# GpSimd's element-wise instructions moved to VectorE in a two-layer hybrid attention, convolution and gating backbone

## The chip, the cores and the metric

The kernel runs on one core of one Trainium2 chip. The metric is device time in microseconds (us) of one execution. The engines are written as in the profile: PE is TensorE, with PEld for its weight loads, DVE is VectorE, ACT is ScalarE, POOL is GpSimd, and SP is SyncE, which issues the DMAs.

## The reference

Two layers work on 1024 latent tokens and 256 context tokens of width 1024. In each layer one combined input projection feeds three mixers: differential attention, a long convolution, and chunked spatial gating. Their outputs are gated, projected, merged and projected once more. Cut to what matters (per layer, latent part):

```python
h = rms_norm(x, norm_pre[l]) * (1.0 + sc[:, None]) + sh[:, None]
z = h @ w_in[l]
q = apply_rope(qk_heads(z[..., COL_Q:COL_GA]), cos, sin)
k = apply_rope(qk_heads(z[..., COL_K:COL_V]), cos, sin)
y_a = diff_head_out(diff_attend(q, k_all, v_all, lam), da_subln[l], lam_init)
filt = hyena_filter(n, hy_f_w1[l], hy_f_b1[l], hy_f_w2[l], hy_f_b2[l], hy_f_w3[l], hy_f_freq[l])
y_b = hyena_branch(z[..., COL_HY:COL_GB], hy_short_w[l], hy_short_b[l], filt, hy_bias[l])   # FFT convolution
y_c = gmlp_branch(z[..., COL_GM:COL_GC], gm_ln_g[l], gm_ln_b[l], gm_ws[l], gm_bs[l])
# merge: out = sum_i sigmoid(gate_i) * ((y_i * silu(g_i)) @ w_branch[l, i]);  out = out @ w_out[l]
x = x + gt[:, None] * rms_norm(out, norm_post[l])
```

The context tokens go through the same weights in the first layer; in the second they only give keys and values.

## The kernel before

Activations lie with channels on the 128 partitions and tokens along the free axis, in three chunks (512, 512 and 256 tokens). All large matmuls are taken as three products of split numbers (`mm3`, L180): high half of the weights by high half of the data, high by low, and low by high, one row of the profile each (L183, L184, L185). So each weight block of 128 x 1024 is loaded by a DMA (`wr`), copied by ACT to its high half `wh` (L103), and its low half is `wl = wr - wh` (L104). `Weights.split_to` does this one block ahead of use, with two buffers each for `wr`, `wh` and `wl`; the subtraction runs on GpSimd, but for some blocks named in `on_vector` on VectorE.

The stages, in order of time: **the start** (0 to 320 us: the long-convolution filters of layer 0, the conditioning and the first normalisation), **attention of layer 0** (to 905), **convolution and gating of layer 0** (to 1420), **merge** (`phase_m`, to 1680), **output** (`phase_o`, to 1870), and the same for layer 1: attention (to 2435), convolution and gating with the filters of layer 1 among them (to 2870), merge (to 3115) and output (to the end).

The change touches element-wise helpers of all these:

- `kvq`: the rotary step on keys and queries. VectorE makes a shuffled copy and a product (L396, L397), GpSimd a product and a sum (L398, L399).
- `filters` (L733), `butterfly` (L641), `fold` (L712): the filter in time (`hb`, L750), its sum of squares (`ssq`, L756), even and odd parts `U` (L760 on VectorE, L761 on GpSimd), then a hand-made radix-8 step (L650) of sums and differences named `Z`, `W` and `o`, most on VectorE, some on GpSimd by their number in `pool_share`. Its results go to PE as `fk` (filters) or `fu` (data), L699 to L704.
- `conv`, `product`, `inverse`, `conv_out`: the data side of the convolution. A short convolution makes `zc` (L791 to L793), a product of two of them (L831) is transposed on PE (`T`, L838).
- `mix` (L1091): the gating. VectorE normalises (`bst`, L193 to L195, `vn`, L1129), PE multiplies (`mm`, L1103), VectorE scales (`mv`, L1134), and GpSimd adds and multiplies (L1136, L1137).
- `phase_m`: products with the gates (`gy`, L1161) and accumulation (`acc`, L1182). `phase_o` and `phase_last`: the residual sum `xt` (L1235, L1325).

What sets the order: the helpers are Python generators that the phases interleave, and a list scheduler then sets each engine's queue when the program is built, from the dependencies and its own estimates. Each engine runs its queue strictly in order, and an instruction that waits for a semaphore holds what stands behind it.

Of the kernel before, what the change touches and what calls it, by code (L numbers as in the profile page):

```python
# [55 lines left out]
class Weights:  # L56


    def __init__(self, nc, pool, order, src):
        self.nc, self.pool, self.order, self.src = nc, pool, order, src  # L60
        self.on_vector = ({("out", 0, 2, d) for d in (1, 3, 5, 7)}
                          | {("br", 1, i, d) for i in range(3) for d in range(KT)})
        self.i = 0
# [106 lines left out]
class Kernel:  # L170
# [185 lines left out]
    def hmod(self, l, c, x):  # L356
# [5 lines left out]
        for k in range(KT):  # L362
# [8 lines left out]
            (nc.gpsimd if k in (1, 3, 5) else nc.vector).tensor_tensor(out=hl[:, k, :], in0=u, in1=hh[:, k, :].bitcast(F32),  # L371
                                                                op=SUB)
# [3 lines left out]
    def kvq(self, l, h, P, psum):  # L376
# [13 lines left out]
        def rope(c, ps):  # L390
# [7 lines left out]
            nc.gpsimd.tensor_tensor(out=sh, in0=sh, in1=St[:, t0:t0 + n], op=MUL)  # L398
            nc.gpsimd.tensor_tensor(out=t1, in0=t1, in1=sh, op=ADD)  # L399
# [241 lines left out]
    def butterfly(self, U, P, ZW, pool_share):  # L641
# [91 lines left out]
    def filters(self, l, q, P, M, psum, ZW):  # L733
# [6 lines left out]
        for i, (b0, b1, st) in enumerate(((0, 2, 1), (1, 3, 1), (4, 6, 2), (7, 5, 1))):  # L740
# [14 lines left out]
            if i:  # L755
                nc.gpsimd.tensor_tensor(out=ss, in0=ss, in1=sq, op=ADD)  # L756
# [115 lines left out]
    def conv_out(self, l, q, t0, n, y, u, x0, nrm):  # L872
# [3 lines left out]
        nc.gpsimd.tensor_tensor(out=y, in0=y, in1=x0, op=MUL)  # L876
# [3 lines left out]
    def inverse(self, Y, yt, M, P, psum):  # L880
# [7 lines left out]
        def tt(out, a, b, op, eng=nc.vector):  # L888
            eng.tensor_tensor(out=out, in0=a, in1=b, op=op)
# [30 lines left out]
        hh = tt(two(), cs[:, 5:7, :], cs[:, 0:4:3, :], SUB, nc.gpsimd)  # L920
# [77 lines left out]
    def ctx_conv(self, l, q, P, M, psum):  # L998
# [3 lines left out]
        nc.gpsimd.tensor_tensor(out=v, in0=v, in1=x1, op=MUL)  # L1002
# [88 lines left out]
    def mix(self, l, P, psum):  # L1091
# [19 lines left out]
        for i in range(nch):  # L1111
# [30 lines left out]
    def phase_m(self, l):  # L1142
        nc = self.nc
        with ExitStack() as st:
# [5 lines left out]
            for i in (0, 2, 1):  # L1150
                gat = {}
                for c in self.chunks(l):
# [3 lines left out]
                    for b in range(4):  # L1156
# [582 lines left out]
```

## Time and profile before

| | |
|---|---|
| median of 3 runs | 3230.13 us (3229.13 to 3231.52) |
| the profiled execution | 3228.0 us |
| its span in the trace | 3226.2 us |
| PE busy | 3016.2 us (93%) |
| VectorE busy | 1809.8 us (56%), 3822 instructions |
| ScalarE busy | 1224.0 us (38%) |
| GpSimd busy | 961.0 us (30%), 640 instructions |
| mean TensorE clock granted | 0.971 of full speed |

The span lies inside the execution; 1.8 us of the profiled execution lie around it. PE's busy time is the sum of its matmuls' time, which is longer where the granted clock is lower. An engine that is not busy waits for another one or for a DMA, or has nothing to do. In the views of waits, a row names the engine and line that waited, what ended the wait, the total in us, the number of waits and the longest.

### The profile page before, as it was taken

The numbers are of one execution on the slowest core, as the hardware profiler recorded it, in microseconds if no ns is written. First come the engines' busy times: TensorE is split into PE (matmuls) and PEld (weight loads), VectorE is DVE, ScalarE is ACT, GpSimd is POOL, SyncE is SP. The second block draws the span as 40 slices with busy tenths as digits, with TensorE's granted clock in tenths as the row PEclk, the third lists the DMA queues.
The fourth block names the chain that finished last, engine by engine and source line by source line (L and its number), as shares of the span: only waits on it lengthen the run. The fifth ranks groups of instructions, "written<-read, shape, count | busy, mean of one in ns | idle before, by whom it ended". The sixth has DMA issues, their size and how long they took to land. (4 is left out here: it accounts for less than half of the span.)

```text
span 3226.2 us, 43742 instructions
## 1 busy us (share of the span) xinstructions
PE 3016.2 (93%) x16220; PEld 2539.3 (79%) x16220; DVE 1809.8 (56%) x3822; ACT 1224.0 (38%) x2037; POOL 961.0 (30%) x640
## 2 busy tenths in 40 slices
PE   8888999999999998999999899999998888899998
PEld 4777878787878787878877778888886766788878
DVE  6754757676865655313355755545466667534344
ACT  5332535353532322223343444535454333323231
POOL 1442020202013333223543321221214544322431
PEclk9899999999999999999999999999999999999999
DMA  6323222222355555435452421221114645546342
GB/s 248 111 81 107 76 72 77 72 77 80 104 186 175 188 168 169 146 127 155 131 163 85 145 70 48 67 64 56 61 60 140 189 157 181 191 144 218 106 134 79
DMA packets 243381, 395.79 MB, mean 123 GB/s; under 512 B 23582, under 2 KB 127902, under 8 KB 241888
## 3 DMA queue, kind: packets, MB, share of 16 engines
q1 hardware_dynamic: 243168, 392.99, 37.7%
q8 instruction: 128, 2.10, 0.3%
q14 instruction: 85, 0.70, 0.1%
HBM read 285.81 MB, written 97.65 MB: 119 GB/s over the span
## 5 line engine op out<-in xcount | busy, mean ns | idle before, releaser
L183 PE MATMUL pd<-hh,wh 128*128 128x512 f32 (+1 forms) x2784 | 1052.2, 378 | 10.5 <-DVE r L397 6.4
L185 PE MATMUL pd<-hh,wl 128*128 128x512 f32 (+1 forms) x2784 | 1037.8, 373 | 2.2 <-POOL wl L104 2.2
L184 PE MATMUL pd<-hl,wh 128*128 128x512 f32 (+1 forms) x2784 | 1037.0, 373 | 0.2 <-DVE hl L371 0.2
L104 POOL TENSOR_TENSOR wl<-wr,wh 128x1024 fp32r<-128x1024 f32 (+1 forms) x177 | 413.9, 2338 | 1374.5 <-ACT wh L103 1284.0
L183 PEld LDWEIGHTS pd<-hh,wh 128*128 128x128 f32 x2784 | 532.4, 191 | 92.1 <-DVE r L397 6.8
L185 PEld LDWEIGHTS pd<-hh,wl 128*128 128x128 f32 x2784 | 531.7, 191 | 87.9 <-POOL wl L104 2.6
L184 PEld LDWEIGHTS pd<-hl,wh 128*128 128x128 f32 x2784 | 532.4, 191 | 78.0 <-DVE hl L371 0.7
L103 ACT ACTIVATE wh<-wr 128x1024 fp32r<-128x1024 f32 (+1 forms) x204 | 194.7, 954 | 230.5 <-PE pd L184 131.2
L463 ACT ACTIVATE e<-S,sm 128x1280 f32<-128x1280 f32 (+1 forms) x144 | 177.7, 1234 | 204.1 <-DVE sm L461 185.0
L460 DVE TENSOR_REDUCE sm<-S 128x1 f32<-128x1280 f32 (+1 forms) x144 | 197.1, 1369 | 74.3 <-PE S L456 73.6
L183 PE MATMUL pb<-gh,wh 128*128 128x512 f32 (+1 forms) x480 | 179.3, 373 | 6.1 <-ACT gh L199 4.7
L185 PE MATMUL pb<-gh,wl 128*128 128x512 f32 (+1 forms) x480 | 179.0, 373 | 4.2 <-POOL wl L104 3.4
L184 PE MATMUL pb<-gl,wh 128*128 128x512 f32 (+1 forms) x480 | 178.7, 372 | 0.2
L456 PE MATMUL S<-K,q 128*128 128x512 f32 (+1 forms) x400 | 149.8, 374 | 14.4 <-ACT e L463 14.3
L293 DVE SCALAR_TENSOR_TENSOR at<-aw,acs 128x256 f32<-128x256 f32 x224 | 116.8, 545 | 46.0 <-DMA aw<-in_ada_wT 39.5
L456 PE MATMUL S<-K,w 128*128 128x512 f32 (+1 forms) x400 | 136.6, 356 | 0.0
L200 DVE TENSOR_TENSOR pl<-T,ph 128x512 fp32r<-128x512 f32 x164 | 109.4, 686 | 34.0 <-ACT ph L199 32.0
L1052 ACT ACTIVATE ev<-pd 128x512 f32<-128x512 f32 (+1 forms) x122 | 66.6, 546 | 156.5 <-PE pd L185 83.5
L199 ACT ACTIVATE ph<-T 128x512 fp32r<-128x512 f32 x164 | 94.3, 596 | 75.4 <-PE T L493 75.3
L1161 DVE TENSOR_TENSOR gy<-gy,gg 128x512 f32<-128x512 f32 (+1 forms) x30 | 22.3, 742 | 163.9 <-DMA gg<-gd 124.5
L1182 POOL TENSOR_TENSOR acc<-acc,sel 128x512 f32<-128x512 f32 (+1 forms) x70 | 86.6, 1251 | 85.1 <-DVE sel L1180 84.9
L456 PEld LDWEIGHTS S<-K,q 128*128 128x128 f32 x400 | 75.9, 190 | 44.4 <-ACT e L463 30.0
(405 smaller groups left out, 5308.1 us busy)
## 6 DMA issues: line engine op xcount, KB each, us to landing
wr<-in_w_in SPq DMA_DIRECT2D x136, 512.0 KB, 3.4
fm<-in_fmat SPq DMA_DIRECT2D x99, 192.0 KB, 3.0
fm<-in_imat SPq DMA_DIRECT2D x72, 256.0 KB, 3.2
sel<-sd SPq DMA_DIRECT2D x70, 256.0 KB, 2.7
aw<-in_ada_wT SPq DMA_DIRECT2D x128, 128.0 KB, 2.5
wr<-in_w_out SPq DMA_DIRECT2D x28, 512.0 KB, 3.3
sd<-ev SPq DMA_DIRECT2D x50, 256.0 KB, 2.0
zd<-zz SPq DMA_DIRECT2D x48, 256.0 KB, 2.0
```

The lines of the kernel that those rows point to most:

```text
L103: nc.scalar.activation(out=hi[:, 0:k, :], in_=t[:, 0:k, :], func=AF.Copy)
L104: eng.tensor_tensor(out=lo[:, 0:k, :], in0=t[:, 0:k, :], in1=hi[:, 0:k, :].bitcast(F32), op=SUB)
L183: mm(out, lhsT=wh, rhs=xh, start=first, stop=False)
L184: mm(out, lhsT=wh, rhs=xl, start=False, stop=False)
L185: mm(out, lhsT=wl, rhs=xh, start=False, stop=last)
L199: nc.scalar.activation(out=hi, in_=src, func=AF.Copy)
L200: nc.vector.tensor_tensor(out=lo, in0=src, in1=hi.bitcast(F32), op=SUB)
L293: nc.vector.scalar_tensor_tensor(out=t, in0=w, scalar=1.0, in1=cs[:, j, :], op0=MUL, op1=MUL, accum_out=sums[:, b, j, i:i + 1])
L456: nc.tensor.matmul(S[:, a - k0:b - k0], lhsT=st[:, o + 128 * t:o + 128 * t + 128], rhs=K[m][:, a:b], start=i == 0, stop=i == 1)
L460: nc.vector.reduce_max(out=sm[:, 0:1], in_=S[:, 0:nk], axis=AX.X)
L463: nc.scalar.activation(out=e[:, 0:nk], in_=S[:, 0:nk], func=AF.Exp, bias=sm[:, 1:2], scale=0.125, accum_out=sm[:, 2:3])
L1182: eng.tensor_tensor(out=acc[c][:, d, :], in0=acc[c][:, d, :], in1=sel[c], op=ADD)
```

## The change

Every `nc.gpsimd.tensor_tensor` becomes an `nc.vector.tensor_tensor` with the same operands. The selections go with it: `on_vector` in `Weights`, `pool_share` in `butterfly`, and the choices by block or by index. Nothing else is edited; tiles, buffers, DMAs, matmuls and the work of ScalarE are the same. The core of the diff:

```diff
 class Weights:
-        self.on_vector = ({("out", 0, 2, d) for d in (1, 3, 5, 7)}
-                          | {("br", 1, i, d) for i in range(3) for d in range(KT)})
...
-            eng = nc.vector if self.order[i] in self.on_vector else nc.gpsimd
             nc.scalar.activation(out=hi[:, 0:k, :], in_=t[:, 0:k, :], func=AF.Copy)
-            eng.tensor_tensor(out=lo[:, 0:k, :], in0=t[:, 0:k, :], in1=hi[:, 0:k, :].bitcast(F32), op=SUB)
+            nc.vector.tensor_tensor(out=lo[:, 0:k, :], in0=t[:, 0:k, :], in1=hi[:, 0:k, :].bitcast(F32), op=SUB)
...
-            nc.gpsimd.tensor_tensor(out=sh, in0=sh, in1=St[:, t0:t0 + n], op=MUL)
-            nc.gpsimd.tensor_tensor(out=t1, in0=t1, in1=sh, op=ADD)
+            nc.vector.tensor_tensor(out=sh, in0=sh, in1=St[:, t0:t0 + n], op=MUL)
+            nc.vector.tensor_tensor(out=t1, in0=t1, in1=sh, op=ADD)
...
-    def butterfly(self, U, P, ZW, pool_share):
+    def butterfly(self, U, P, ZW):
...
-            eng = nc.gpsimd if cnt[0] in pool_share else nc.vector
-            eng.tensor_tensor(out=out, in0=a, in1=b, op=op)
+            nc.vector.tensor_tensor(out=out, in0=a, in1=b, op=op)
...
-                nc.gpsimd.tensor_tensor(out=ss, in0=ss, in1=sq, op=ADD)
+                nc.vector.tensor_tensor(out=ss, in0=ss, in1=sq, op=ADD)
...
-            nc.gpsimd.tensor_tensor(out=u[:, :, 128:256], in0=hb[:, :, 0, :], in1=hb[:, :, 1, :], op=SUB)
+            nc.vector.tensor_tensor(out=u[:, :, 128:256], in0=hb[:, :, 0, :], in1=hb[:, :, 1, :], op=SUB)
...
-            nc.gpsimd.tensor_tensor(out=o, in0=o, in1=bs, op=ADD)
-            nc.gpsimd.tensor_tensor(out=o, in0=o, in1=u, op=MUL)
+            nc.vector.tensor_tensor(out=o, in0=o, in1=bs, op=ADD)
+            nc.vector.tensor_tensor(out=o, in0=o, in1=u, op=MUL)
...
-                        (nc.gpsimd if b % 2 else nc.vector).tensor_tensor(out=y, in0=y, in1=g, op=MUL)
+                        nc.vector.tensor_tensor(out=y, in0=y, in1=g, op=MUL)
...
-                            eng = nc.vector if i == 1 and d >= KT - 2 else nc.gpsimd
-                            eng.tensor_tensor(out=acc[c][:, d, :], in0=acc[c][:, d, :], in1=sel[c], op=ADD)
+                            nc.vector.tensor_tensor(out=acc[c][:, d, :], in0=acc[c][:, d, :], in1=sel[c], op=ADD)
...
-                    (nc.vector if k % 2 else nc.gpsimd).tensor_tensor(out=xt[:, k, :], in0=ot[:, k, :], in1=xt[:, k, :], op=ADD)
+                    nc.vector.tensor_tensor(out=xt[:, k, :], in0=ot[:, k, :], in1=xt[:, k, :], op=ADD)
```

The same edit is made in `hmod` (L371), `fold`, `product` (L810), `conv_out` (L876), `inverse` (six of its sums), `ctx_conv` (L1002) and `phase_last` (L1325). In the built program GpSimd keeps the four MEMSETs of constants at the very start and nothing else; its 636 TENSOR_TENSOR instructions stand on VectorE, whose queue grows from 3566 to 4202 instructions. The scheduler also reorders the queues, so line numbers in the rows of the changed program are those of the new file (some 3 to 9 lower).

VectorE's queue in the start stage, before, from the filter in time `hb` of one filter to the sums `o` that PE's next transform `fk` reads:

```order
L750 TENSOR_TENSOR hb<-fh,dec 128x512
L638 TENSOR_TENSOR fw3l<-fw_1278,fw3h 128x256
L760 TENSOR_TENSOR U<-hb 128x2x128
L650 TENSOR_TENSOR o_1229<-U 128x512
L650 TENSOR_TENSOR Z<-U 128x512 x2
L650 TENSOR_TENSOR W<-Z 128x768 x2
L650 TENSOR_TENSOR o_1235<-Z,U 128x512
L650 TENSOR_TENSOR o_1237<-o_1235,o_1229 128x512
```

The same place after:

```order
L754 TENSOR_TENSOR U<-hb 128x2x128
L749 TENSOR_TENSOR ssq<-ssq,sqf 128x512
L643 TENSOR_TENSOR Z<-U 128x512
L707 TENSOR_TENSOR ssq<-ssq 128x256
L643 TENSOR_TENSOR Z<-U 128x512
L708 TENSOR_TENSOR ssq<-ssq 128x128
L643 TENSOR_TENSOR W<-Z 128x768 x2
L643 TENSOR_TENSOR o_1229<-U 128x512
L643 TENSOR_TENSOR o_1231<-U 128x512
L643 TENSOR_TENSOR o_1235<-Z,U 128x512
L101 TENSOR_TENSOR wl<-wr,wh 128x1024
L643 TENSOR_TENSOR o_1237<-o_1235,o_1229 128x512
```

The second part of `U` (L754), the sum of squares and its folds (L749, L707, L708) have come between, and so has the low half `wl` of a weight block, ahead of the last sum.

VectorE's queue in the convolution and gating of layer 1, before, up to `vn`, which PE's gating matmul `mm` reads:

```order
L650 TENSOR_TENSOR W<-Z 128x768
L193 TENSOR_TENSOR bst<-bst 128x1
L650 TENSOR_TENSOR W<-Z 128x768
L194 SCALAR_TENSOR_TENSOR bst<-bst 128x1
L792 SCALAR_TENSOR_TENSOR zc<-z,cols,zc 128x1023
L195 SCALAR_TENSOR_TENSOR bst<-bst 128x1
L650 TENSOR_TENSOR o_21827<-Z,U 128x512
L1129 TENSOR_SCALAR vn<-vn,bst 128x512
```

The same place after:

```order
L708 TENSOR_TENSOR ssq<-ssq 128x128
L190 TENSOR_TENSOR bst<-bst 128x1
L643 TENSOR_TENSOR Z<-U 128x512
L191 SCALAR_TENSOR_TENSOR bst<-bst 128x1
L643 TENSOR_TENSOR Z<-U 128x512
L192 SCALAR_TENSOR_TENSOR bst<-bst 128x1
L643 TENSOR_TENSOR W<-Z 128x768
L1122 TENSOR_SCALAR vn<-vn,bst 128x512
L643 TENSOR_TENSOR W<-Z 128x768
L643 TENSOR_TENSOR o_21821<-U 128x512
L643 TENSOR_TENSOR o_21823<-U 128x512
```

The second `W`, which stood ahead of `vn`, stands behind it now, as do the short-convolution step `zc` and the sum `o_21827`, further on; the last fold of `ssq` has come ahead of it.

VectorE's queue in the output of layer 0, before, in the residual tail of one chunk, while PE works on the next chunk's blocks:

```order
L1233 SCALAR_TENSOR_TENSOR ot<-ot,mod_4467,mrb 128x512 x2
L1235 TENSOR_TENSOR xt<-ot,xt 128x512
L1260 TENSOR_TENSOR ss<-ss,sq 128x512
L1233 SCALAR_TENSOR_TENSOR ot<-ot,mod_4467,mrb 128x512
L1235 TENSOR_TENSOR xt<-ot,xt 128x512
L1260 TENSOR_TENSOR ss<-ss,sq 128x512
L328 TENSOR_TENSOR ss<-ss,sq 128x512 x7
```

The same place after:

```order
L1227 TENSOR_TENSOR xt<-ot,xt 128x512
L1225 SCALAR_TENSOR_TENSOR ot<-ot,mod_4467,mrb 128x512 x2
L1227 TENSOR_TENSOR xt<-ot,xt 128x512 x2
L1225 SCALAR_TENSOR_TENSOR ot<-ot,mod_4467,mrb 128x512
L101 TENSOR_TENSOR wl<-wr,wh 128x1024
L1227 TENSOR_TENSOR xt<-ot,xt 128x512
L1252 TENSOR_TENSOR ss<-ss,sq 128x512
L325 TENSOR_TENSOR ss<-ss,sq 128x512
L101 TENSOR_TENSOR wl<-wr,wh 128x1024
L325 TENSOR_TENSOR ss<-ss,sq 128x512 x5
```

All sums `xt` are on this queue now, and the low halves `wl` of the following blocks stand behind scalings `ot`, sums `xt` and sums of squares `ss` of the tail.

## Rows read from the trace of the kernel before

**Rows 1.** The page's head: span, busy time of each engine.
```profile
span 3226.2 us, 43742 instructions
PE 3016.2 (93%) x16220; PEld 2539.3 (79%) x16220; DVE 1809.8 (56%) x3822; ACT 1224.0 (38%) x2037; POOL 961.0 (30%) x640
```

**Rows 2.** Windows: window, length, busy us of each engine, clock, DMA share, GB/s.
```profile
core 0: us, PE busy (x) PEld busy (x) DVE busy (x) ACT busy (x) POOL busy (x), PEclk, DMA share, GB/s
1870.00:2435.00 565.00, 562.78 (x3046) 471.55 (x3045) 302.00 (x620) 272.16 (x404) 117.03 (x60) 1.00 0.19 61
2435.00:2870.00 435.00, 375.12 (x1994) 311.86 (x1993) 288.29 (x544) 146.66 (x253) 191.93 (x142) 0.95 0.55 175
```

**Rows 3.** Waits of PE in the start (0 to 320 us): total, times, longest.
```profile
PE fk L699 <- DVE o L650: 15.6, 3, 5.6
...
PE pd L185 <- POOL wl L104: 2.2, 1, 2.2
...
PE fk L700 <- DVE o L650: 2.2, 1, 2.2
```

**Rows 4.** Waits of PE in the convolution of layer 0 (905 to 1420 us).
```profile
PE T L838 <- DVE zc L831: 10.7, 2, 5.4
PE fk L699 <- DVE cu L979: 8.9, 3, 4.2
```

**Rows 5.** Waits of PE in the output of layer 0 (1680 to 1870 us).
```profile
PE po L185 <- POOL wl L104: 6.1, 1, 6.1
PE msq L209 <- DVE ss L328: 5.5, 1, 5.5
```

**Rows 6.** Waits of PE in the convolution of layer 1 (2435 to 2870 us).
```profile
PE T L838 <- DVE zc L831: 17.6, 2, 12.4
PE mm L1103 <- DVE vn L1129: 15.5, 4, 7.1
PE fk L699 <- issue: 10.2, 2, 9.8
```

**Rows 7.** By form, POOL and DVE: shapes, count, busy us, mean ns, idle before.
```profile
L104 POOL TENSOR_TENSOR wl<-wr,wh 128x1024 fp32r<-128x1024 f32 x153 | 382.9, 2503 | 1324.1 <-ACT wh L103 1248.7 <-PE S L456 42.5 <-PE T L493 24.9
L1182 POOL TENSOR_TENSOR acc<-acc,sel 128x512 f32<-128x512 f32 x56 | 76.4, 1371 | 85.1 <-DVE sel L1180 84.9
L1180 DVE TENSOR_TENSOR sel<-pb,sel 128x512 f32<-128x512 f32 x64 | 43.9, 687 | 64.1 <-PE pb L185 61.7 <-ACT wh L103 2.1
L650 DVE TENSOR_TENSOR Z<-U 128x512 f32<-128x512 f32 x32 | 46.7, 1484 | 2.6 <-POOL U L761 2.4
```

**Rows 8.** Timeline, DVE and POOL in the convolution of layer 1: start, length, instruction.
```profile
2473.00 2.59 POOL L104 TENSOR_TENSOR wl<-wr,wh 128x1024 fp32r<-128x1024 f32 x1
2473.97 2.17 DVE L650 TENSOR_TENSOR Z<-U 128x512 f32<-128x512 f32 x1
...
2478.18 0.68 DVE L650 TENSOR_TENSOR Z<-U 128x512 f32<-128x512 f32 x1
...
2484.78 0.95 DVE L650 TENSOR_TENSOR W<-Z 128x768 f32<-128x768 f32 x1
...
2655.74 1.21 DVE L831 TENSOR_TENSOR zc<-zc 128x1024 f32<-128x1024 f32 x1
```

**Rows 9.** Timeline, DVE and PE in the start; in brackets the idle time before.
```profile
140.16 0.69 DVE L750 TENSOR_TENSOR hb<-fh,dec 128x512 f32<-128x512 f32 x1 [2.87 <-PE fh L747]
...
152.71 1.29 DVE L650 TENSOR_TENSOR o<-o,o 128x512 f32<-128x512 f32 x2
...
153.55 0.76 PE L699 MATMUL fk<-o,fm 128*128 128x128 f32 x2 [5.62 <-DVE o L650]
```

**Rows 10.** Windows before and after the stall of PE at 2488 us.
```profile
2461.30:2488.10 26.80, 17.75 (x86) 14.38 (x86) 26.60 (x39) 11.44 (x18) 19.20 (x13) 0.92 0.34 106
2488.20:2494.00 5.80, 5.80 (x34) 5.47 (x35) 5.80 (x5) 0.73 (x3) 3.81 (x2) 0.50 0.27 87
```

**Rows 11.** Waits of all engines, the longest row: POOL for ACT's high halves.
```profile
POOL wl L104 <- ACT wh L103: 1284.0, 126, 36.6
```

More of the change, by code (lines that the diff above doesn't have):

```diff
@@ L370, in hmod @@
             nc.scalar.activation(out=hh[:, k, :], in_=u, func=AF.Copy)
-            (nc.gpsimd if k in (1, 3, 5) else nc.vector).tensor_tensor(out=hl[:, k, :], in0=u, in1=hh[:, k, :].bitcast(F32),
-                                                                op=SUB)
+            nc.vector.tensor_tensor(out=hl[:, k, :], in0=u, in1=hh[:, k, :].bitcast(F32), op=SUB)
         self.hT[c] = (hh, hl)
@@ L712, in fold @@
     def fold(self, s):
-        self.nc.gpsimd.tensor_tensor(out=s[:, 0, :, :], in0=s[:, 0, :, :], in1=s[:, 1, :, :], op=ADD)
-        self.nc.gpsimd.tensor_tensor(out=s[:, 0, 0, :], in0=s[:, 0, 0, :], in1=s[:, 0, 1, :], op=ADD)
+        self.nc.vector.tensor_tensor(out=s[:, 0, :, :], in0=s[:, 0, :, :], in1=s[:, 1, :, :], op=ADD)
+        self.nc.vector.tensor_tensor(out=s[:, 0, 0, :], in0=s[:, 0, 0, :], in1=s[:, 0, 1, :], op=ADD)
     def norm_of(self, ss, out, psum, P):
@@ L760, in filters @@
             nc.vector.tensor_tensor(out=u[:, :, 0:128], in0=hb[:, :, 0, :], in1=hb[:, :, 1, :], op=ADD)
-            nc.gpsimd.tensor_tensor(out=u[:, :, 128:256], in0=hb[:, :, 0, :], in1=hb[:, :, 1, :], op=SUB)
+            nc.vector.tensor_tensor(out=u[:, :, 128:256], in0=hb[:, :, 0, :], in1=hb[:, :, 1, :], op=SUB)
             yield 1.5
-        for i, (pp, ab) in enumerate(zip(self.GROUPS, self.butterfly(U, P, ZW(), (8, 16, 18)))):
+        for i, (pp, ab) in enumerate(zip(self.GROUPS, self.butterfly(U, P, ZW()))):
             yield 1.0
@@ L809, in product @@
         nc.vector.tensor_tensor(out=y[:, :, 0, :], in0=t1[:, :, 0, :], in1=t1[:, :, 1, :], op=SUB)
-        nc.gpsimd.tensor_tensor(out=y[:, :, 1, :], in0=t2[:, :, 0, :], in1=t2[:, :, 1, :], op=ADD)
+        nc.vector.tensor_tensor(out=y[:, :, 1, :], in0=t2[:, :, 0, :], in1=t2[:, :, 1, :], op=ADD)
     def conv(self, l, q, M, psum):
@@ L847, in conv @@
                     ZW = [F.tile([128, n, 128], F32, name="ZW"[n == 6]) for n in (8, 6)]
-                    for i, (pp, ab) in enumerate(zip(self.GROUPS, self.butterfly(U, F, ZW, (4, 6, 8, 10)))):
+                    for i, (pp, ab) in enumerate(zip(self.GROUPS, self.butterfly(U, F, ZW))):
                         kt = F.tile([128, 2, 2, 128], F32, name="kt", tag="kt")
@@ L875, in conv_out @@
         nc.vector.scalar_tensor_tensor(out=y, in0=u, scalar=self.col(f"hyb{l}", q), in1=y, op0=MUL, op1=ADD)
-        nc.gpsimd.tensor_tensor(out=y, in0=y, in1=x0, op=MUL)
+        nc.vector.tensor_tensor(out=y, in0=y, in1=x0, op=MUL)
         nc.sync.dma_start(out=self.yd[l][:, q, t0:t0 + n], in_=y)
@@ L886, in two, with tt @@
             return P.tile([128, 2, 128], F32, name="i2", tag="o2")
-        def tt(out, a, b, op, eng=nc.vector):
-            eng.tensor_tensor(out=out, in0=a, in1=b, op=op)
+        def tt(out, a, b, op):
+            nc.vector.tensor_tensor(out=out, in0=a, in1=b, op=op)
             return out
@@ L919, in inverse @@
         gg = tt(two(), cs[:, 1:3, :], cs[:, 4:8:3, :], ADD)
-        hh = tt(two(), cs[:, 5:7, :], cs[:, 0:4:3, :], SUB, nc.gpsimd)
+        hh = tt(two(), cs[:, 5:7, :], cs[:, 0:4:3, :], SUB)
         cm, cx = two(), two()
@@ L939, in inverse @@
         tt(hh, hh, tt(two(), cm, mb, SUB), ADD)
-        tt(mf, mf, cx, ADD, nc.gpsimd)
+        tt(mf, mf, cx, ADD)
         tt(y[1], gg[:, 0, :], gg[:, 1, :], ADD)
-        tt(y[7], gg[:, 0, :], gg[:, 1, :], SUB, nc.gpsimd)
+        tt(y[7], gg[:, 0, :], gg[:, 1, :], SUB)
         tt(y[3], hh[:, 1, :], hh[:, 0, :], SUB)
@@ L1001, in ctx_conv @@
         v = self.short_conv(l, 8 + q, SEQ, CTX, P, "o2", None, "o2")
-        nc.gpsimd.tensor_tensor(out=v, in0=v, in1=x1, op=MUL)
+        nc.vector.tensor_tensor(out=v, in0=v, in1=x1, op=MUL)
         yield 2.0
@@ L1324, in tail @@
                                                        scalar=gg[:, k + i, 0:1], in1=r, op0=MUL, op1=MUL)
-                        nc.gpsimd.tensor_tensor(out=xt[:, i, :], in0=ot[:, k + i, :], in1=xt[:, i, :], op=ADD)
+                        nc.vector.tensor_tensor(out=xt[:, i, :], in0=ot[:, k + i, :], in1=xt[:, i, :], op=ADD)
                     nc.sync.dma_start(out=self.A["outT"][:, k:k + 2, :], in_=xt)
```

6 lines of the change are left out of this document (2 added, 4 removed).

## The prediction

> **What bounds the kernel now.** I read the page's head first. The span is 3226.2 us and PE is busy for 3016.2 of it [rows 1], so PE sets the time, and all that element-wise work can change is the 210 us in which PE stands idle and the stretches in which its clock is lowered. VectorE is busy for 56% and GpSimd for 30% [rows 1]: neither is the bound over the whole span. Next the windows by stage [rows 2]. In the attention of layer 1, PE is idle for 2.2 of 565 us; there nothing can be gained, only lost. In the convolution and gating of layer 1 it is idle for 60 of 435 us, and there VectorE is busy for 288 and GpSimd for 192. Then the waits of PE, stage by stage [rows 3 to 6]: nearly all large ones end on VectorE (`o`, `cu`, `zc`, `ss`, `vn`) and few on GpSimd itself (`wl`, 2.2 and 6.1 us). So the question is whether VectorE delivers these few results earlier or later once it also has GpSimd's work.
>
> Two rows say how the engines share. Uncontended, VectorE takes 0.69 us for 128x512 (`sel<-pb`), and GpSimd 1.37 us for the same shape; at 128x1024 it is 1.21 us against 2.50 [rows 7, 8]. But VectorE's own sums are slow beside GpSimd: the same `Z<-U` took 2.17 us while GpSimd made a `wl`, and 0.68 us a little later; its mean over 32 is 1.48 us [rows 7, 8]. So part of the time that VectorE shows as busy is waiting for GpSimd, and it comes back when GpSimd is silent.
>
> That is what the Trainium skill says in "SBUF — State Buffer", section "Who interferes with whom": GpSimd's ports are VectorE's second pair, and a VectorE instruction with two SBUF inputs contends with a GpSimd instruction that reads SBUF. The 2.17 against 0.68 us agrees.
>
> **Instructions.** GpSimd's 636 instructions take 961 us. At the ratios of the two shapes above (0.48 and 0.50) VectorE needs 0.49 x 961 = 470 us for them. What comes back is bounded by 32 x (1.48 - 0.68) = 26 us, the `Z` group alone, and by 961 - 470 = 491, if GpSimd lost nothing but what VectorE lost too; I take 200, since other groups show the same lengthening. VectorE is then busy for 1810 + 470 - 200 = 2080 us, 64%, between 1789 and 2254. It doesn't become the bound of the whole, so the sum goes by single stalls.
>
> **The start.** `fk` waits three times for `o`, 15.6 us in all, once 2.2 more, and a projection 2.2 us for `wl` [rows 3]. One case closely: from the start of `hb` at 140.16 to the end of the first of the two last sums `o` (152.71 + 0.65) pass 13.2 us [rows 9]. In the order after, what stands from `hb` to the first sum `o_1237` is, in uncontended durations, eight instructions of 128x512 (two `Z`, `hb`, `ssq`, three `o` and that sum, 0.69 each), four of half that width (taken at 0.42, between half of 0.69 and the whole), one fold of 0.3, two `W` of 0.95 and a `wl` of 1.21: 10.6 us, plus 1 us for ScalarE's part, which the sums need and which now has less cover. That gains 1.6 us. PE's own queue puts this `fk` eight matmuls later, 8 x 0.185 = 1.5 us at the mean of a stage without stalls (562.78 us over 3046) [rows 2]. So 5.6 becomes 2.5; three such cases give 3 x 3.1 = 9.3 us, and the two small waits go whole, 4.4: **-14 us**, bounds -4 (the small ones alone) and -20 (all).
>
> **Convolution of layer 0.** `T` waits twice for `zc` (10.7 us) and `fk` three times for the context's `cu` (8.9) [rows 4]. By the count of matmuls ahead of them in PE's new queue the two `T` stand 1.4 and 3.9 us later; less contention adds some 3. The `cu` are not helped by order. **-8 us**, bounds 0 and -19.6.
>
> **Output of layer 0.** `msq` waits 5.5 us for a chain of `ss`, and `po` 6.1 us for a `wl` that GpSimd makes [rows 5]. In the new order I add up 19.7 us of VectorE work ahead of `ss` where 23.8 us passed: 4 us gained, and a `wl` is made 1.3 us faster: **-5 us**. Against that, six `wl` of this stage now stand behind the tail's `ot`, `xt` and `ss` (third order pair), two or three instructions of 0.69 us each, 1.8 us per block: **+11 us**. Bounds 0 (the one block ahead hides it) and +25 (six instructions each).
>
> **Attention.** VectorE gets 1.21 us for each `wl` and four times 0.69 for each pair of rotary steps. PE's queue ran there with 2.2 us of idle time, and VectorE is busy for 302 of 565 us [rows 2]; the work is taken up by the other 263 us. I count nothing, with a rival below for the case that it isn't.
>
> **Convolution of layer 1.** `T` waits 17.6 us for `zc`, `mm` 15.5 for `vn`, and `fk` 10.2 where the profile shows no releaser [rows 6]. For `vn` at 2488: 26.8 us passed, of which VectorE was busy for 26.6 in 39 instructions beside 19.2 us of GpSimd [rows 10]. In the order after, the instructions of the same stretch add up to 20.0 us uncontended, although 13 of GpSimd's are among them, because `W`, `zc` and `o` have moved behind `vn` and nothing is contended. So `vn` comes 6.8 us earlier and its longest wait of 7.1 goes; the next, of some 6, goes because PE stands 9 us later there: -13. For `zc` at 2657, 30.1 us become 22.5, but PE arrives 3.6 us earlier: 4 of 12.4, and 1 of the other: -5. The `fk` of 9.8 us stands 7 us later in PE's queue against 2.6 us more work on VectorE: -4. Together **-22 us**, bounds -8 (half of `vn` alone) and -43.3 (all).
>
> **The clock.** After the stall of 2488 the granted clock is 0.50 for 5.8 us with PE busy throughout, and that is the lower level, 1.2 GHz [rows 10]; it costs 2.9 us. Five of the stalls above (two small ones of the start, one `T`, two `vn`) go nearly whole: **-15 us**, bounds -5 and -58 (all 20 stalls of [rows 3 to 6]).
>
> **Sum:** 3228.0 - 14 - 8 - 5 + 11 - 22 - 15 = 3175 us for the profiled execution. It lay 2 us under the median, within its runs' spread, and I leave that out.
>
> **The rivals.** *Nothing comes back.* VectorE in its full stretches gains nothing: GpSimd's instructions only queue on it, where they ran beside it before. Then only PE's direct waits for GpSimd go, 2.2 and 6.1 us [rows 3, 5] with 2.9 us of clock each: 3228 - 14 = 3214. For it speaks that VectorE is busy without a gap before the worst stalls (26.6 of 26.8 us) [rows 10]; against it the 2.17 beside 0.68 us [rows 8]. The Trainium skill has this as a warning: "Perfetto Trace Analysis", section "Optimizing Scalar/DVE Operations", says that moving operations between these two engines might not help, because of the shared port. By that page the time would be this rival's.
>
> *Slower, by waiting in line.* GpSimd waited 126 times, 10 us each and 1284 us in all, for ScalarE's `wh` [rows 11]. It had nothing behind it that was urgent. VectorE takes over these waits in its queue, and behind them stand the row maxima and sums of the attention, on which PE's next scores depend. If in half of the 126 the queue is held for 1.5 us beyond PE's slack, 63 x 1.5 = 95 us come on top of gains of 50: 3228 + 95 - 50 = 3273. It decides from about 0.8 us per such wait. Against it: in the new order these `wl` mostly stand behind an instruction that ended within 3 us of `wh` in the trace before, and PE uses them 8 to 30 us later; for it: the scheduler's estimates are not the chip's.
>
> *All stalls go.* If VectorE is freed by more than I take, all of [rows 3 to 6] goes: 20.0 + 19.6 + 11.6 + 43.3 = 94.5 us, and the clock after 10 to 20 stalls, 29 to 58: 3075 to 3104, say 3090. Against it: `cu` and two `zc` have no slack in the new order.
>
> That the change doesn't do what it says is excluded by the built program: GpSimd keeps four MEMSETs.
>
> **How the numbers follow.** A difference under 0.2%, 6.5 us, can hardly be told from none here. Forecast 0.60, nothing back 0.17, all stalls 0.11, slower 0.12. The forecast's own terms give 3105 to 3215. The range reaches from 3085, through most of the third rival, to 3225, past the first; it leaves out the slower one and a few per cent below. Faster by over 0.2%: 0.60 + 0.11 + most of 0.17 = 0.81; within: 0.07, from the first rival with half of the waiting in line; slower: 0.12.
>
> **What would show it.** Right: `Z<-U` at a mean near 0.69 us, VectorE busy near 2080 us, `vn` waits under 3 us, `fk` waits in the start near 2 us. The first rival: the waits of [rows 3, 6] as long as before with VectorE full ahead of them. The second: a row of VectorE's `wl` waiting for `wh` and PE's idle time in 1870 to 2435 far above 2 us. Wrong altogether: VectorE's sums as slow as before without GpSimd, or new waits of PE for `wl` above 25 us.

## The result and the profile after

The changed kernel takes 3039.3 us (median of 4 runs, 3036.5 to 3040.7) against 3230.8 us for the kernel before on the same chip: a ratio of 0.9405, 95% interval 0.9389 to 0.9421. On another chip the ratio was 0.9417 (0.9398 to 0.9437). The forecast was 3175 us in a range of 3085 to 3225: right in sign, but the gain of 191 us is more than three times the forecast one of 53, and it lies below the range.

The page's head, after, answers to [rows 1]:

```profile
span 3039.0 us, 43277 instructions
PE 2964.2 (98%) x16220; PEld 2501.2 (82%) x16220; DVE 1944.0 (64%) x4458; ACT 1225.0 (40%) x2037; POOL 0.2 (0%) x4
```

PE's idle time fell from 210.0 to 74.8 us, and its busy time by 52 us with the same 16220 matmuls, because the granted clock is at the lower level more rarely (mean 0.992 in place of 0.971). By the clock records of the two traces PE works at the lower level (granted 0.5, 1.2 GHz) for 137 us before and 40 after; half of the difference, 48 us, is nearly the whole fall of its busy time. VectorE has 636 instructions more and only 134 us of busy time more.

Three windows of before, the start, the attention and the convolution of layer 0, which [rows 2] doesn't have (window, length, busy us of PE, PEld, DVE, ACT, POOL, clock, DMA share, GB/s):

```profile
0.00:320.00 320.00, 274.47 (x1436) 219.91 (x1436) 192.50 (x365) 116.25 (x202) 110.24 (x77) 0.93 0.40 137
320.00:905.00 585.00, 559.41 (x3215) 478.48 (x3216) 414.40 (x1119) 277.79 (x449) 91.66 (x49) 0.98 0.26 81
905.00:1420.00 515.00, 482.26 (x2727) 411.98 (x2726) 247.18 (x600) 145.43 (x270) 154.90 (x122) 0.98 0.52 168
```

The windows after, cut at the same matmuls as the stages of before; the last row of the table, merge and output of layer 1, is the rest of the span:

```profile
0.00:275.90 275.90, 259.04 (x1437) 208.03 (x1438) 187.45 (x441) 116.66 (x203) 0.20 (x4) 0.98 0.47 159
275.90:834.40 558.50, 550.30 (x3208) 470.37 (x3207) 420.36 (x1158) 276.64 (x448) 0.00 (x0) 1.00 0.27 84
834.40:1314.50 480.10, 471.40 (x2735) 404.23 (x2734) 272.75 (x729) 146.95 (x271) 0.00 (x0) 1.00 0.56 181
1314.50:1561.30 246.80, 245.09 (x1262) 210.16 (x1261) 145.47 (x243) 87.80 (x161) 0.00 (x0) 0.99 0.50 150
1561.30:1745.50 184.20, 170.78 (x845) 144.82 (x844) 121.21 (x240) 74.74 (x128) 0.00 (x0) 0.94 0.38 129
1745.50:2309.20 563.70, 563.13 (x3046) 470.84 (x3045) 351.97 (x679) 271.42 (x405) 0.00 (x0) 1.00 0.19 61
2309.20:2692.70 383.50, 366.33 (x1993) 303.77 (x1992) 278.03 (x685) 145.90 (x253) 0.00 (x0) 0.99 0.63 199
```

| stage | before | after | gain | forecast (clock apart) |
|---|---|---|---|---|
| start | 320.0 | 275.9 | 44.1 | 14 |
| attention, layer 0 | 585.0 | 558.5 | 26.5 | 0 |
| convolution and gating, layer 0 | 515.0 | 480.1 | 34.9 | 8 |
| merge, layer 0 | 260.0 | 246.8 | 13.2 | 0 |
| output, layer 0 | 190.0 | 184.2 | 5.8 | -6 |
| attention, layer 1 | 565.0 | 563.7 | 1.3 | 0 |
| convolution and gating, layer 1 | 435.0 | 383.5 | 51.5 | 22 |
| merge and output, layer 1 | 356.2 | 346.3 | 9.9 | 0 |

The forecast's 15 us for the clock were not divided among the stages; the measured gains contain it. Over the whole span the forecast was 38 us less idle time of PE and 15 us for the clock; measured are 135 us less idle time and 52 us less busy time. In the convolution of layer 1, VectorE now makes 685 instructions in 278 us where it made 544 in 288 [rows 2]: with more work it is busy for less time.

Long waits of PE in the whole span, after (total, times, longest):

```profile
PE S L452 <- ACT e L459: 6.8, 5, 2.3
PE fk L692 <- DMA fm<-in_fmat: 5.8, 8, 1.5
PE po L180 <- ACT wh L100: 5.7, 4, 3.2
...
PE mrb L215 <- DVE mn L192: 3.6, 3, 2.3
PE T L831 <- DVE zc L824: 3.6, 3, 2.0
PE po L182 <- DVE wl L101: 3.5, 3, 2.8
PE msq L206 <- DVE ss L325: 3.4, 1, 3.4
```

Of the waits in [rows 3 to 6] most are gone: `fk` for `o` (15.6 us in the start) is 1.3 us in the whole span, `T` for `zc` (28.3 in both layers) 3.6, and no wait of `mm` for `vn` or of `fk` for `cu` is left. In the output of layer 0 `msq` no longer waits for `ss` (the 3.4 us above are in the start), but `po` still waits 3.5 us for `wl`.

VectorE's forms after, answering to [rows 7] (count, busy us, mean ns):

```profile
L101 DVE TENSOR_TENSOR wl<-wr,wh 128x1024 fp32r<-128x1024 f32 x156 | 190.6, 1222 | 175.5 <-ACT wh L100 172.0 <-PE mrb L215 2.7 <-PE pd L182 0.2
L1174 DVE TENSOR_TENSOR acc<-acc,sel 128x512 f32<-128x512 f32 x64 | 44.2, 690 | 1.4
L1173 DVE TENSOR_TENSOR sel<-pb,sel 128x512 f32<-128x512 f32 x64 | 44.1, 689 | 34.9 <-PE pb L182 34.7
L643 DVE TENSOR_TENSOR Z<-U 128x512 f32<-128x512 f32 x32 | 21.5, 687 | 0.0
```

`Z<-U` took 1484 ns in the mean and takes 687; the mean of all 32 is now that of the fastest before. `sel<-pb`, which has one operand in PSUM, took 687 ns before and takes 689: it was never lengthened. VectorE makes `wl` in 1.22 us and `acc` in 0.69 where GpSimd took 2.50 and 1.37 [rows 7].

### The profile page after: what moved, and what is told of

It reads as the page before. It is cut to its first block, busy times and chain, and to the rows that moved or that the text cites. A ratio compares the mean times of both kernels' runs of the same rounds, so it can differ in the third digit from the quotient of the medians.

```text
span 3039.0 us, 43277 instructions
## 1 busy us (share of the span) xinstructions
PE 2964.2 (98%) x16220; PEld 2501.2 (82%) x16220; DVE 1944.0 (64%) x4458; ACT 1225.0 (40%) x2037; POOL 0.2 (0%) x4
## 4 chain that ended last, share of the span: by engine, by line
PE 85%; DVE 7%; DMA 6%; ACT 1%; issue 1%; SPq 0%; DVEq 0%; ACTq 0%
PE pd L180 16%; PE pd L182 16%; PE pd L181 16%; PE S L452 5%; PE pb L181 3%; PE pb L182 3%; PE pb L180 3%; PE T L489 2%; PE po L182 2%; PE po L180 2%; PE po L181 2%; PE ip L703 2%; DMA aw<-in_ada_wT 2%; PE O L180 1%; PE O L181 1%; PE O L182 1%
## 5 line engine op out<-in xcount | busy, mean ns | idle before, releaser
L101 DVE TENSOR_TENSOR wl<-wr,wh 128x1024 fp32r<-128x1024 f32 (+1 forms) x204 | 223.6, 1096 | 209.6 <-ACT wh L100 206.0
L459 ACT ACTIVATE e<-S,sm 128x1280 f32<-128x1280 f32 (+1 forms) x144 | 177.7, 1234 | 178.0 <-DVE sm L457 143.8
L181 PE MATMUL pb<-gl,wh 128*128 128x512 f32 (+1 forms) x480 | 177.7, 370 | 0.4 <-DVE gl L197 0.3
L290 DVE SCALAR_TENSOR_TENSOR at<-aw,acs 128x256 f32<-128x256 f32 x224 | 88.5, 421 | 40.6 <-DMA aw<-in_ada_wT 37.9
L468 DVE SCALAR_TENSOR_TENSOR e<-e,sm,e 128x1280 f32<-128x1280 f32 (+1 forms) x72 | 102.7, 1426 | 6.2 <-ACT e L467 5.7
L489 PE MATMUL T<-ident,e 128*128 128x128 f32 x656 | 104.3, 276 | 0.6 <-DVE pl L197 0.3
```

What stands on the lines that cost most here:

```text
L101: nc.vector.tensor_tensor(out=lo[:, 0:k, :], in0=t[:, 0:k, :], in1=hi[:, 0:k, :].bitcast(F32), op=SUB)
L181: mm(out, lhsT=wh, rhs=xl, start=False, stop=False)
L459: nc.scalar.activation(out=e[:, 0:nk], in_=S[:, 0:nk], func=AF.Exp, bias=sm[:, 1:2], scale=0.125, accum_out=sm[:, 2:3])
L468: nc.vector.scalar_tensor_tensor(out=e0[:, 0:nk], in0=e0[:, 0:nk], scalar=s0[:, 3:4], in1=e[:, 0:nk], op0=MUL, op1=ADD)
L489: nc.tensor.transpose(T[:, 256 * i + 128 * t:256 * i + 128 * t + 128], e[t][:, 128 * (2 * g + i):128 * (2 * g + i) + 128], self.ident)
```

## The experiments

Three theories stood against each other. **Contention**: GpSimd, whenever it reads SBUF, holds VectorE's instructions that have two SBUF inputs, and the gain is VectorE's own time come back. (In this kernel PSUM holds what PE's matmuls write, and SBUF all other tiles.) **Path**: GpSimd's instructions are slow and stand, with a hop between engines on either side, in the chains that PE waits for. **Order**: the build's scheduler set another order, and that removed the stalls. For differences of a run to the kernel after I take 0.941 of the kernel before, between the two ratios measured for it, some 3035 us.

### A load on GpSimd that nothing waits for

The kernel after with additions on GpSimd, issued at the start, that write a tile nobody reads. The queues of all other engines are, instruction for instruction, those of the kernel after, so order and path can't differ.

```diff
+                scr = P.tile([128, 128], F32, name="scr")
+                for _ in range(400):
+                    nc.gpsimd.tensor_tensor(out=scr, in0=self.ones, in1=self.ones, op=ADD)
                 fh = self.filter_hidden(0, P, psum)
```

> The kernel after, with 400 additions of 128x128 on GpSimd at the start that read two SBUF operands and write a tile nobody reads; nothing waits for them, and the queues of PE, VectorE, ScalarE and SyncE are the same, instruction for instruction, as in the kernel after. Contention theory (a VectorE sum with two SBUF inputs is held while GpSimd reads SBUF): VectorE's sums of the start grow from 0.69 us to 1 us or more, PE's waits for `o` and `hb` come back, the start grows from 276 us by 15 to 45 us, the other stages stay, total 3054 to 3085. Path theory (the gain is that GpSimd's slow instructions and the hops to and from them are off the path) and order theory (the gain is the scheduler's new order): 3039 within 6 us.

Measured: 0.9469 (0.9455 to 0.9483), 19 us slower than the kernel after. The start takes 299.0 us in place of 275.9; the other stages are those of the kernel after within 4 us each. The additions run from 1 to 253 us. The second kernel has MEMSETs in place of the additions, which write SBUF and read nothing:

```diff
+                for _ in range(600):
+                    nc.gpsimd.memset(scr, 0.0)
```

> The same with 600 MEMSETs of 128x128 on GpSimd, which write SBUF and read nothing. Contention theory with reads alone: 3039 within 6 us. Contention by writes too: 10 to 40 us more. Path and order theory: 3039 within 6 us.

Measured: 0.9401 (0.9385 to 0.9416), the time of the kernel after; the start takes 277.7 us. The MEMSETs end at 161 us. The third has the same number of elements to read in half as many instructions of twice the width (`scr` of 128x256, 200 additions). It differs from the first in two more things, the type of `scr`, bf16, and the inputs, `ones` read twice over:

```diff
+                scr = P.tile([128, 2, 128], mybir.dt.bfloat16, name="scr")
+                one = self.ones.unsqueeze(1).to_broadcast([128, 2, 128])
+                for _ in range(200):
+                    nc.gpsimd.tensor_tensor(out=scr, in0=one, in1=one, op=ADD)
```

> The kernel after, with 200 additions on GpSimd at the start of 128x256 in place of 400 of 128x128: the same number of elements read, in instructions of twice the length; nothing waits for them and all other queues are those of the kernel after. If a VectorE instruction is held for a whole GpSimd instruction, each wait is longer, up to GpSimd's one instruction, but there are half as many to wait for: the start 290 to 305 us as with 400 short ones (299), and VectorE's small 128x1 sums show single lengths near one GpSimd instruction. If the holding were by element, spread evenly, every VectorE sum would be longer by the same factor and none of the small ones by as much as one GpSimd instruction. Path and order theory: 276 us.

Measured: 0.9523 (0.9509 to 0.9537), 36 us slower than the kernel after; the start takes 313.2 us, near the 320 of the kernel before. I had expected 290 to 305: this load costs more than I thought, although GpSimd was busy with it for less time (it ends at 179 us). That it is the length of the instructions, and not the type, isn't shown by itself. By form, GpSimd's load and two groups of VectorE in the start, 400 short additions:

```profile
L1471 POOL TENSOR_TENSOR scr<-ones 128x128 f32<-128x128 f32 x400 | 220.9, 552 | 31.9 <-DVE ones L1456 0.6
...
L643 DVE TENSOR_TENSOR Z<-U 128x512 f32<-128x512 f32 x16 | 13.5, 861 | 0.0
L743 DVE TENSOR_TENSOR hb<-fh,dec 128x512 f32<-128x512 f32 x16 | 11.0, 689 | 23.9 <-PE fh L740 23.9
L192 DVE SCALAR_TENSOR_TENSOR mn<-mn 128x4 f32<-128x4 f32 x6 | 1.5, 253 | 0.1
```

600 MEMSETs:

```profile
L1471 POOL MEMSET scr<- 128x128 f32 x600 | 125.5, 209 | 34.7 <-POOLq L1721 0.3
...
L743 DVE TENSOR_TENSOR hb<-fh,dec 128x512 f32<-128x512 f32 x16 | 11.0, 689 | 28.1 <-PE fh L740 28.1
L643 DVE TENSOR_TENSOR Z<-U 128x512 f32<-128x512 f32 x16 | 10.6, 683 | 0.0
L192 DVE SCALAR_TENSOR_TENSOR mn<-mn 128x4 f32<-128x4 f32 x6 | 1.0, 161 | 0.1
```

200 additions of twice the width:

```profile
L1472 POOL TENSOR_TENSOR scr<-ones 128x256 bf16<-128x256 f32 x200 | 162.1, 810 | 16.2 <-DVE ones L1456 0.6
...
L643 DVE TENSOR_TENSOR Z<-U 128x512 f32<-128x512 f32 x16 | 13.1, 840 | 0.0
L743 DVE TENSOR_TENSOR hb<-fh,dec 128x512 f32<-128x512 f32 x16 | 11.0, 688 | 27.7 <-PE fh L740 27.7
L192 DVE SCALAR_TENSOR_TENSOR mn<-mn 128x4 f32<-128x4 f32 x6 | 2.1, 348 | 0.1
```

`Z` has both inputs in SBUF and grows from 0.69 to 0.86 us under the first load. Under the third the mean of 0.84 mixes two kinds: the 8 that start while the load runs take 0.99 us, the 8 after it 0.69. Under writes `Z` stays at 0.68, also the 9 of 16 that start while the MEMSETs run. `hb` reads `fh` from PSUM and stays at 0.69 us under every load. The tiny `mn` of 128x4 grows from 0.16 to 0.25 and 0.35 us in the mean; single ones take 0.37 us beside the short additions and 0.57 beside the long ones. So what it is held for goes by GpSimd's instruction, not by its own length. PE's waits of `fk` for `o` come back, 8.7 us and 6.3 us in the two loads with reads, none under the MEMSETs. With equal queues, contention alone makes the start 23 and 37 us longer. These loads keep GpSimd busy for 221 and 162 us, where the kernel before had 110 us in the start, so they show that contention can cost as much as the 44 us gained there, not how many of the 44 it was. The Trainium skill's "SBUF — State Buffer", section "Who interferes with whom", says that an instruction of VectorE with two SBUF inputs contends with a GpSimd instruction that reads SBUF and not with one that only writes it, and that one with at most one SBUF input, outside the two-port modes, doesn't contend; these rows agree with all three.

### Parts of the change alone

The low halves `wl` alone moved (the kernel before with `eng = nc.vector` in `split_to`), and everything but `wl` moved (the kernel after with the choice of engine for `wl` as before):

```diff
-            eng = nc.vector if self.order[i] in self.on_vector else nc.gpsimd
+            eng = nc.vector
```

> The kernel before, with the low halves `wl` alone moved to VectorE. They are 383 + 31 of GpSimd's 961 us. Contention theory: about 40% of the gain of 191 us, so near 3155 us. Path theory: `wl` is made 10 to 30 us ahead of use, and PE waited for it 12 us in all, so 3205 to 3220. Order theory: no figure, but a gain without shorter VectorE sums.

> The kernel after, with the low halves `wl` alone back on GpSimd. Contention theory: about 40% of the gain is lost, near 3115 us. Path theory: 12 to 25 us are lost, 3051 to 3064 us.

Measured: 0.9695 (0.9680 to 0.9709) with `wl` alone, 98 us faster than before where contention had said 75 and path 10 to 25; and 0.9637 (0.9622 to 0.9651) with all but `wl`, 73 us slower than the kernel after where contention had said 76 and path 12 to 25. `wl` is 52% of the gain of 190 us by the first and 38% by the second, and it is the part whose results PE hardly waited for (11.7 us for GpSimd's `wl` in the whole span of before). Both runs also have an order of their own; what the order alone is worth was not measured. By stage it is clearest in the attention of layer 0, where two thirds of GpSimd's 91.7 us are 25 `wl`: 559.5 us with `wl` alone moved, 585.5 with all but `wl` moved, against 558.5 and 585.0 for the kernels after and before. So the whole gain of that stage is `wl`, and moving the other 24 instructions of GpSimd there, sums and products of the rotary step, gave nothing. Waits of PE there, all but `wl` moved:

```profile
PE S L455 <- ACT e L462: 15.4, 5, 3.3
PE mrb L218 <- DVE mn L195: 6.0, 3, 2.1
```

`wl` alone moved:

```profile
PE S L456 <- ACT e L463: 5.1, 4, 2.2
PE mrb L218 <- DVE mn L195: 4.9, 3, 1.9
```

Next, two small parts put back on GpSimd in the kernel after: first what stands in PE's chains (the second half of `U` and the share of the butterfly), then what PE doesn't need soon (the sums of squares and folds):

```diff
-            nc.vector.tensor_tensor(out=u[:, :, 128:256], in0=hb[:, :, 0, :], in1=hb[:, :, 1, :], op=SUB)
+            nc.gpsimd.tensor_tensor(out=u[:, :, 128:256], in0=hb[:, :, 0, :], in1=hb[:, :, 1, :], op=SUB)
...
+            eng = nc.gpsimd if cnt[0] in pool_share else nc.vector
```

> The kernel after, with the second halves of `U` and the share of the butterfly back on GpSimd as in the kernel before (96 of its 961 us), all of them in the chain that ends in PE's `fk` and `fu`. Contention alone, by share of GpSimd's time: 10% of 190 us, so 15 to 22 us slower than after. If standing in the chain matters as well: 30 to 50 us slower, with waits of PE for GpSimd's `o` and `U`.

```diff
-                nc.vector.tensor_tensor(out=ss, in0=ss, in1=sq, op=ADD)
+                nc.gpsimd.tensor_tensor(out=ss, in0=ss, in1=sq, op=ADD)
...
```

> The kernel after, with the sums of squares `ssq` and their folds back on GpSimd (62 of 961 us). Nothing that PE needs soon follows from them. Contention: 6% of 190 us, 8 to 14 us slower than after, in the start and the convolution of layer 1. Path theory: within 3 us of after.

Measured: 0.9468 (0.9453 to 0.9483) with the chain's part back, 19 us slower than the kernel after for 107 us of GpSimd; 0.9461 (0.9441 to 0.9481) with the part off the chains back, 16 us slower for 60 us of GpSimd. In the start alone the second costs 13.5 us more than the kernel after needs there (289.4 us), the first 11.0 (286.9). Per microsecond that GpSimd works the part in the chains costs 0.18 us, the part outside them 0.27, `wl` (73 over 432) 0.17 and the whole (190 over 961) 0.20. The intervals of the two small parts are wide, some 6 and 7 us either way, so they can't be told apart; what they do exclude is that work off the chains is free (path had said within 3 us) and that work in the chains costs 30 us or more. PE did wait 7.3 us for GpSimd's `o` in the first, so the path exists; it is not what sets the price. The second lies 2 us past its expected 8 to 14 us, which is within its interval.

### Half of one group of sums back on GpSimd

In the output of layer 0 the forecast had named a new wait: the low halves `wl` behind the tail's sums on VectorE. That stage is the one that gained least among those with stalls, 184.2 us, and with `wl` alone moved it took 178.2. So half of the residual sums `xt` go back to GpSimd there, as in the kernel before:

```diff
-                    nc.vector.tensor_tensor(out=xt[:, k, :], in0=ot[:, k, :], in1=xt[:, k, :], op=ADD)
+                    (nc.vector if k % 2 else nc.gpsimd).tensor_tensor(out=xt[:, k, :], in0=ot[:, k, :], in1=xt[:, k, :], op=ADD)
```

> The kernel after, with the even ones of the residual sums `xt` in the output of layer 0 back on GpSimd (16 us). There, VectorE's tail stands ahead of the low halves `wl` of the next blocks, and with `wl` alone on VectorE this stage took 178 us against 184 in the kernel after. If the line in front of `wl` is what this stage waits for: 4 to 7 us faster than after. If contention with GpSimd's sums outweighs it: as after or up to 5 us slower.

Measured: 3027.1 us, 0.9388 (0.9374 to 0.9403). To compare on one chip, the kernel after, this one, and one with all of these `xt` on GpSimd:

> The kernel after itself, on the same chip as the two that follow, as the base for them. 3030 to 3040 us, 0.940 of the kernel before.

> The kernel after with the even residual sums `xt` of layer 0's output on GpSimd, beside the kernel after on the same chip. If the line on VectorE ahead of `wl` is what that stage waits for: 5 to 8 us under the kernel after, all of it in the output of layer 0. Otherwise within 3 us.

> The same with all residual sums `xt` of layer 0's output on GpSimd. If only the line on VectorE counts: as fast as with half of them, or faster. If holding VectorE counts more: 3 to 8 us slower than with half of them, as twice as many GpSimd sums read SBUF beside VectorE's tail.

Measured: 3033.0 us (0.9417, 0.9398 to 0.9437), 3026.0 (0.9399, 0.9383 to 0.9415) and 3039.0 (0.9437, 0.9421 to 0.9454). The intervals of the first two overlap, so that the half version is faster as a whole isn't shown by the ratios alone. But of the 8.9 us between the two profiled spans 6.6 lie in the one stage edited, whose windows are, in this order:

```profile
1560.20:1744.50 184.30, 170.72 (x844) 144.73 (x844) 121.14 (x240) 74.73 (x128) 0.00 (x0) 0.94 0.37 129
```
```profile
1556.80:1734.50 177.70, 166.69 (x845) 141.64 (x844) 116.10 (x228) 74.47 (x127) 16.20 (x12) 0.97 0.38 134
```
```profile
1557.30:1748.20 190.90, 173.57 (x844) 148.44 (x844) 118.31 (x216) 74.56 (x127) 31.13 (x24) 0.92 0.36 127
```

184.3, 177.7 and 190.9 us; the stage took 176.2 in the first run of the half version. With half the sums on GpSimd, `po`'s waits for `wh` and `wl` in this stage fall from 9.2 to 5.8 us, and it is busy for 4 us less at a higher clock. That a shorter line on VectorE ahead of `wl` is the reason fits this, but no row shows it directly. With all of the sums on GpSimd the stage is 13 us slower than with half, where I had expected 3 to 8: the `ss` sums take 0.77 us in the mean in place of 0.69, and PE waits 5.1 us for `ss` again. So in this stage a small amount of work on GpSimd, 16 us, still earned something, and 31 us cost more than it gave.

## Why the prediction was wrong

**What was right.** That PE is the bound; that VectorE doesn't become it; that VectorE's sums come back to their uncontended length; that no new wait of weight grows in the attention of layer 1 (idle 2.2 us before, 0.6 after). VectorE is busy for 64% of the span, as forecast, but that is luck: forecast were 2080 us of 3228, and 1944 of 3039 came. The forecast's sign of proof, `Z<-U` near 0.69 us, came. The rival of waiting in line is there, but did PE no harm in the attention of layer 1: VectorE waited for `wh` 73 times, 206 us in all, where GpSimd had waited 126 times and 1284 us [rows 11].

```profile
DVE wl L101 <- ACT wh L100: 206.0, 73, 12.6
```

The rival that all stalls go was the nearest, and at 3090 us still 51 too high: the four stages that it counted gained 136 us, where it had 138. The rival that nothing comes back gave 3214, 175 us off; only the slower one, 3273, is farther. For that rival spoke the warning in the Trainium skill's "Perfetto Trace Analysis", section "Optimizing Scalar/DVE Operations", that moving work between these two engines might not help; in this direction, from GpSimd to VectorE, the runs don't bear it out. GpSimd's reads held VectorE's sums, and with GpSimd silent `Z` takes 0.69 us.

**The step that failed first: attention and merge at zero.** The prediction read PE's idle time in the attention of layer 1, 2.2 us, and put both attentions at nothing by it; the merge and the last stages have no term in the sum, and no reason is given. But in the attention of layer 0 PE was idle for 25.6 of 585 us before and for 8.2 of 558.5 after. Its two largest waits there, before, are in none of the prediction's rows:

```profile
PE S L456 <- ACT e L463: 14.3, 5, 4.7
PE mrb L218 <- DVE mn L195: 9.9, 5, 2.2
```

The stage gained 26.5 us, the merge of layer 0 13.2 and the last stages 9.9, together 50 us, which is what the third rival lacked. The mechanism was in the prediction, a VectorE sum lengthened beside GpSimd, but only as the mean of large sums (`Z`, 1.48 us), and with no row of a small one. In fact an instruction is held for the rest of GpSimd's whole instruction, however small it is itself. In the trace of before, 46 of VectorE's sums and products of at most 8 columns began while a GpSimd instruction ran. 42 of them ended 11 to 20 ns after that instruction's end, up to 2.36 us long, and the other 4 began in its last 0.16 us; the 684 that began beside no GpSimd instruction took at most 0.17 us. The timeline of before in the attention of layer 0, GpSimd, VectorE, PE:

```profile
422.02 2.38 POOL L104 TENSOR_TENSOR wl<-wr,wh 128x1024 fp32r<-128x1024 f32 x1 [28.93 <-ACT wh L103]
```
```profile
421.99 0.16 DVE L193 TENSOR_TENSOR mn<-mn 128x2 f32<-128x2 f32 x1
422.19 2.23 DVE L194 SCALAR_TENSOR_TENSOR mn<-mn 128x2 f32<-128x2 f32 x1
424.45 0.16 DVE L195 SCALAR_TENSOR_TENSOR mn<-mn 128x2 f32<-128x2 f32 x1
...
425.62 0.16 DVE L195 SCALAR_TENSOR_TENSOR mn<-mn 128x2 f32<-128x2 f32 x1
```
```profile
425.93 1.19 PE L218 MATMUL mrb<-ident,mn 128*128 128x128 f32 x4 [2.22 <-DVE mn L195]
```

A step of 128x2, which takes 0.16 us, took 2.23 because a `wl` began 0.17 us before it. PE, which needs the last step of this chain (425.62), stood idle for 2.22 us, so this one `wl` cost PE nearly its own length. Behind an idle time the clock can fall, as in [rows 10]; the stage's clock rose from 0.98 to 1.00. The wait of `S` for ScalarE's `e` is largely VectorE's delay passed on: `e` itself waits for VectorE's `sm`, in this stage before and after

```profile
ACT e L463 <- DVE sm L461: 102.2, 54, 5.9
```
```profile
ACT e L459 <- DVE sm L457: 77.6, 50, 5.4
```

and the wait of `S` fell from 14.3 to 5.1 us when `wl` alone left GpSimd, with ScalarE as busy there as before (277.4 us for 277.8).

**The start, the convolutions: remnants that didn't stay.** For `fk` in the start I worked out 10.6 us for VectorE's instructions from `hb` to the first last sum, 1 us more for ScalarE, and a wait of 2.5 us that remains. After:

```profile
128.45 0.69 DVE L743 TENSOR_TENSOR hb<-fh,dec 128x512 f32<-128x512 f32 x1 [2.56 <-PE fh L740]
...
135.41 0.69 DVE L643 TENSOR_TENSOR o<-Z,U 128x512 f32<-128x512 f32 x1
136.02 1.22 DVE L101 TENSOR_TENSOR wl<-wr,wh 128x1024 fp32r<-128x1024 f32 x1
137.15 1.29 DVE L643 TENSOR_TENSOR o<-o,o 128x512 f32<-128x512 f32 x2
```
```profile
137.98 0.46 PE L692 MATMUL fk<-o,fm 128*128 128x128 f32 x2
```

The order is as in the pair shown ahead of the prediction, but from 128.45 to 137.8 pass 9.4 us, not 11.6. Back to back, an instruction begins 0.61 us after one of 0.69 (135.41 to 136.02) and 1.13 after a `wl` of 1.22: durations overlap, and I had added them up. ScalarE's part was covered. With 2.2 us less, the wait that was to remain is gone: `fk` follows at 137.98 without idle time. In the convolutions, too, waits that I had left standing went. In that of layer 1 I took 22 of the 43.3 us of listed waits, and PE's idle time fell by 43 (59.9 to 17.2); in that of layer 0 I took 8 of 19.6, and it fell by 24 (32.7 to 8.7). How much of this belongs to which wait stays open.

For VectorE's whole work the 470 us were right: in the trace of after, the durations of the 636 moved instructions add up to 470. What comes back was mis-sized: the durations of VectorE's other instructions fell by some 275 us, where I took 200. And 61 us more of all durations overlap, which I had left out. So VectorE's busy time rose by 134 us and not by 270.

**The output of layer 0: right in kind, too dear.** The stage gained 5.8 us where I had -6; the waits for `wl` behind the tail exist (3.5 us), and taking half of the sums `xt` out of VectorE's tail brings 7 to 8 us. No run here shows the +11 us as such.

**The clock.** 15 us were forecast, from five stalls at 2.9 us each; PE's busy time fell by 52. The term followed the stalls and was wrong with them: with most stalls gone, most of the clock's share came back, 48 of the 68 us that the 137 us at the lower level had cost.

**The range.** It should have reached to 3040: the third rival was priced from the waits in the rows that I had listed, not from PE's whole idle time of 210 us and its clock, and so its end was not the end. The 3105 to 3215 given for the forecast's own terms don't come out of their bounds either, which add up to 3082 at the good ends and 3231 at the bad ones; even 3082 is 43 us above the measured time. And the profiled execution, 3228.0, lay 1.1 us below the lowest of the runs listed with it, not within them.

## What to carry to other kernels

Before giving element-wise work to GpSimd, look in the timeline for small VectorE instructions that last as long as a GpSimd instruction beside them; each is VectorE's queue standing still, and in this kernel most of PE's waits that followed were booked on VectorE or ScalarE, not on GpSimd. Work that is "off the path" on GpSimd isn't free: here each microsecond of it cost the kernel about 0.2 us, whether or not anybody waited for its result. When such contention ends, bound the gain by the whole idle time of the bounding engine and its lost clock, here 210 and 68 us; put no stage at nothing before its own idle time is read; and add VectorE's work by the distance of starts, not by durations.

## What the runs showed of the hardware

GpSimd reading SBUF held VectorE's instructions with two SBUF inputs to the end of its own instruction (128x2: 0.16 us became 2.23 beside a `wl` of 2.38). The same number of elements in half as many GpSimd instructions, with another type and access, cost the start 37 in place of 23 us. GpSimd's MEMSETs held nothing (0.68 us for `Z`), and VectorE's sums with one PSUM input were never held (0.69 us for `hb` under every load). VectorE's back-to-back sums of 128x512 begin every 0.61 us while each lasts 0.69.
